# A decoder layer's MoE stage: the norm's per-feature factor moved from the token rows into the experts' gate and up weights

## The chip, the cores and the metric

The kernel runs on one core of a Trainium2 chip. The metric is device time in microseconds (us) of one execution, the median of several. The core has a matrix engine (TensorE, **PE** in the rows; its weight loads are **PEld**), a vector engine (VectorE, **DVE**), an activation engine (ScalarE, **ACT**), a general engine (GpSimd, **POOL**) and a queue that issues transfers (SyncE, **SP**); 16 DMA engines move data between device memory and the on-chip memories (SBUF, and PSUM for matmul results). Each engine executes its own list of instructions in order and waits on the others through semaphores.

## What is computed

A decoder layer on x (1024 tokens x 1024 features): two mixers in parallel (a convolution branch and forgetting attention), cross-attention into 256 memory tokens, then a mixture of 16 experts of which each token uses two. The change touches only the norm ahead of the experts and the experts' first matmuls:

```python
def rmsnorm(x, g):
    y = x * lax.rsqrt(jnp.mean(x * x, axis=-1, keepdims=True) + EPS)
    return y * g

# inside the layer
h = rmsnorm(x, norm_moe_g)                       # g: one factor per feature
g_star = argmax(softmax(h @ wg + bg))            # one of 4 groups
e_sel = (h @ we + be)[group g_star]              # its 4 experts, top 2 are used
a = jnp.einsum("nd,edf->nef", hf, w_gate)
b = jnp.einsum("nd,edf->nef", hf, w_up)
u = jax.nn.silu(a) * b * combine[..., None]
x = x + jnp.einsum("nef,efd->nd", u, w_down)
```

Since h = (x r) g with r one number per token and g one per feature, the factor g may stand on the rows of h or on the rows of w_gate and w_up.

## The kernel before, in words

Matmuls are made exact enough by splitting both operands: `split` (L132 to L138) writes a high part with ACT (`hi`, L134, optionally times `scale`) and the remainder `lo` with DVE (L138) or, for some weights, POOL (L136); `mm3` (L140 to L144) then issues three matmuls per tile. The order of each engine's list is made by a scheduler ahead of time, from the order in the code, priorities (`high_priority`) and explicit "issue after" marks; free buffers limit how far ahead something may stand.

The stages in order of time: the mixers, the output projection, cross-attention (`xa_q`, `xa_attend`, `xa_out`), then routing and experts. Tokens go in two halves of 512. `xa_out(n)` (L768) computes half n of the cross-attention output with eight weight tiles; it transposes the result back to token rows x3 (PE L781, ACT L783), and sums their squares (DVE L784). `rows_of` (L903) makes the norm's factor r from these sums (a chain of small DVE instructions, L907 and L165 to L150, called n3v, n3t, n3r), corrects the router's logits with it (L910, L911), and writes the normed rows to device memory. For the first half ACT multiplies x3 by r (L925) and POOL by the factors of the features, `grow` (L926); for the second half POOL multiplies by `grow` ahead of time (`gained`, L819, tiles hg) and ACT by r once it is known (L918). `route` then picks the experts (DVE L953 to L982, result M), places the tokens with small matmuls (PE L986 to L989), computes the slots of the tokens in each expert's list (Am on DVE, `slot_sums` on PE, L1081), and from these the indices `ids`. With `ids`, POOL issues the indirect transfers that gather an expert's rows (`fetch`, L1305); PE transposes them (L1251), ACT and DVE split the transposes (xgT), PE multiplies them with the split weights `gu` (L142 to L144).

Two experts, 0 and 1, are handled early: their first 128 rows come from the first half of the tokens alone, so that their matmuls can run while the second half is routed. The other 14 follow in a loop (L1490 on): load the raw weights (SP, L1407), split them (`gu_weights`, L1194, tiles of 128x1024; four for gate and up, two for down, per expert), gather, transpose, multiply, and add to the output by an indirect transfer (L1352). A short second list of each of these experts uses the unsplit weights: its transposes are copied by ACT (`turn`, L1316, tile xgL).

The router's weights `wr` already carry g (L876). The tile `grow` was filled by a transfer on POOL's queue (L880); its buffer is used again by `gfin`, the factors of the final norm, loaded by SP (L1512).

Of the kernel before, what the change touches and what calls it, by code (L numbers as in the profile page):

```python
# [7 lines left out]
F32 = mybir.dt.float32  # L8
# [8 lines left out]
P = 128  # L17
# [38 lines left out]
def half(n):  # L56
    return slice(n * HALF, n * HALF + HALF)


def blk(i):  # L60
    return slice(i * P, i * P + P)
# [3 lines left out]
def layer_kernel(ctx, tc, a, out, dbg=None):  # L65
# [700 lines left out]
    st, HG = {}, {}  # L766

    def xa_out(n):  # L768
# [19 lines left out]
        for m in range(KD):  # L788
# [5 lines left out]
            if m == 4:  # L794
                for k in range(4):
                    products(k)
                rows(0)
                if n:
                    HG[0] = gained(0)
# [10 lines left out]
        if n:  # L810
            HG[1] = gained(1)
        return ss

    def gained(b):

        tiles = [xt_p.tile([P, 2, HALF], F32, name=f"hg{b}", tag=("xt1a", "xt1b")[b], bufs=2) for _ in range(2)]
        hg = [x[:, i] for x in tiles for i in range(2)]
        for t in range(4):
            G.tensor_tensor(hg[t], x3[4 + t][:, half(b)], grow[:, half(b)], op=OP.mult)  # L819
        return hg  # L820
# [58 lines left out]
    grow = ro.tile([P, D], F32, name="grow", tag="grow", bufs=1)  # L879
    G.dma_start(grow, bcast_rows(a["moe_g_row"], D))  # L880
# [22 lines left out]
    def rows_of(hf, ss, htile=None):  # L903
# [10 lines left out]
        for i in range(H4):  # L914
            if hf:
                for b in range(2):
                    h = HG[b][i]
                    A.activation(h, h, AF.Copy, scale=r[:, i:i + 1])  # L918
                    nc.sync.dma_start(h3_dram[blk(t0 + i), half(b)], h)
                continue  # L920
            h = htile()
            if i in ():
                V.scalar_tensor_tensor(h, x3[t0 + i], r[:, i:i + 1], grow, op0=OP.mult, op1=OP.mult)
            else:
                A.activation(h, x3[t0 + i], AF.Copy, scale=r[:, i:i + 1])  # L925
                G.tensor_tensor(h, h, grow, op=OP.mult)  # L926
            nc.sync.dma_start(h3_dram[blk(t0 + i)], h)
# [266 lines left out]
    def gu_weights(src, tile_, raw_=raw_tile, parts=range(4), raws=None):  # L1194
        gu = [[], [], []]
        for b in parts:
# [6 lines left out]
            split(t[0], t[1], raw)  # L1203
# [24 lines left out]
    with pool("rows") as rw:  # L1228
# [7 lines left out]
        lg0 = rows_of(0, ss0, lambda: rw.tile([P, D], F32, name="h3s", tag="h3s", bufs=2))  # L1236
# [4 lines left out]
        with tc.high_priority(offset=600):  # L1241
            lg1 = rows_of(1, ss1)
# [65 lines left out]
    def turn(e, h):  # L1308
        if is_shared(e) and h == 1:
# [6 lines left out]
            A.activation(XT[e, h], pt, AF.Copy)  # L1316
# [194 lines left out]
    gfin = ro.tile([P, D], F32, name="gfin", tag="grow", bufs=1)  # L1511
# [212 lines left out]
```

## Time and profile before

| | before |
|---|---|
| median of 3 runs | 1228.31 us (1223.48 to 1232.91) |
| the profiled execution, own time | 1228.64 us |
| span in the profile | 1226.9 us |
| mean granted TensorE clock | 0.985 of full speed |
| busy: PE / DVE / ACT / POOL | 1159.0 (94%) / 843.0 (69%) / 629.3 (51%) / 404.5 us (33%) |

The span is the time in which the engines work; some 1.7 us of the execution lie around it. A busy engine is one that executes something; the engine with the largest share is where to look for the bound, and the stretches in which it is idle tell what it waited for. "Granted clock" is the share of TensorE's full clock (2.4 GHz) that it was given; 0.5 is 1.2 GHz. Rows of a timeline give the start, the duration, engine, line of the kernel, operation, output and inputs; brackets give the idle time of the engine just before, and what ended it.

### The profile page before, as it was taken

The page shows a single profiled execution, that of the slowest core. Times are in us where ns is not written, and L with a number is a line of the kernel's source. Part 1 is how long each engine was busy: PE and PEld are TensorE (multiplying, and loading weights), DVE is VectorE, ACT ScalarE, POOL GpSimd, SP SyncE. Part 2 cuts the span into 40 slices and gives each one's busy share as a digit, 9 for nine tenths or more (in the row PEclk, how much of TensorE's full clock was granted, in tenths as well). Part 3 has the DMA queues.
Part 4 walks back from the last instruction along what each step waited for, and adds up shares of the span by engine and source line. Part 5 has one row for each costly group of instructions (what it writes and reads, how often), then busy time and mean ns, then how long its engine had stood idle before and what let it go on. Part 6 is the DMA issues. An engine that isn't in the chain of part 4 may idle for free. (4 is left out here: it accounts for less than half of the span.)

```text
span 1226.9 us, 17120 instructions
## 1 busy us (share of the span) xinstructions
PE 1159.0 (94%) x6173; PEld 908.7 (74%) x6174; DVE 843.0 (69%) x1569; ACT 629.3 (51%) x1059; POOL 404.5 (33%) x276
## 2 busy tenths in 40 slices
PE   7999999999999999999999999999977898999995
PEld 3678887878877777788888788788754666667773
DVE  5499998653969787791235754755997784766665
ACT  6345664442646555471333342733742575767765
POOL 3327996221010100101012665273034133233433
PEclk9999999999999999999999999999998898999998
DMA  5211224136111111111343453144356889999967
GB/s 208 75 37 52 58 97 156 51 106 231 53 57 44 44 59 46 39 55 46 103 163 129 155 167 111 66 123 121 101 192 243 270 243 300 301 292 311 320 169 285
DMA packets 57467, 174.12 MB, mean 142 GB/s; under 512 B 7992, under 2 KB 11080, under 8 KB 57376
## 3 DMA queue, kind: packets, MB, share of 16 engines
q1 hardware_dynamic: 49680, 149.76, 36.5%
q0 software_dynamic: 7696, 23.20, 8.1%
q8 instruction: 51, 0.84, 0.3%
q14 instruction: 40, 0.33, 0.1%
HBM read 136.92 MB, written 36.01 MB: 141 GB/s over the span
## 5 line engine op out<-in xcount | busy, mean ns | idle before, releaser
L136 POOL TENSOR_TENSOR w_lo<-w_raw,w_hi 128x1024 fp32r<-128x1024 f32 x58 | 140.1, 2415 | 463.4 <-ACT w_hi L134 453.6
L144 PE MATMUL ps_lin<-hh,w_lo 128*128 128x512 f32 x560 | 221.4, 395 | 2.5 <-POOL w_lo L136 2.5
L142 PE MATMUL ps_lin<-hh,w_hi 128*128 128x512 f32 x560 | 223.0, 398 | 0.7 <-DVE u L357 0.6
L143 PE MATMUL ps_lin<-hl,w_hi 128*128 128x512 f32 x560 | 221.5, 396 | 0.0
L134 ACT ACTIVATE w_hi<-w_raw 128x1024 fp32r<-128x1024 f32 (+1 forms) x100 | 92.1, 921 | 201.0 <-PE ps_lin L143 169.1
L144 PEld LDWEIGHTS ps_lin<-hh,w_lo 128*128 128x128 f32 x560 | 105.3, 188 | 24.6 <-POOL w_lo L136 4.6
L142 PEld LDWEIGHTS ps_lin<-hh,w_hi 128*128 128x128 f32 x560 | 105.4, 188 | 23.3 <-issue 2.9
L143 PEld LDWEIGHTS ps_lin<-hl,w_hi 128*128 128x128 f32 x560 | 105.4, 188 | 21.5 <-issue 1.6
L379 DVE SCALAR_TENSOR_TENSOR ps_cva<-u,dw_w,ps_cva 128x1024 f32<-128x1024 f32 x90 | 111.6, 1280 | 0.5
L138 DVE SCALAR_TENSOR_TENSOR gu<-e_raw,gu 128x1024 fp32r<-128x1024 f32 x64 | 77.5, 1222 | 4.5 <-ACT gu L134 0.8
L375 POOL TENSOR_TENSOR oc<-oc,pj 128x512 f32<-128x512 f32 x60 | 75.8, 1303 | 8.8 <-ACT pj L374 8.7
L134 ACT ACTIVATE gu<-e_raw 128x1024 fp32r<-128x1024 f32 x64 | 67.4, 1058 | 8.0 <-PE ps_lin L144 7.4
L142 PE MATMUL ps_lin<-gu,xgT 128*128 128x512 f32 x144 | 58.8, 408 | 4.1 <-ACT xgT L134 4.1
L374 ACT ACTIVATE pj<-u,dw_w 128x512 f32<-128x512 f32 x60 | 42.4, 721 | 34.3 <-POOL oc L375 34.2
L138 DVE SCALAR_TENSOR_TENSOR dn<-d_raw,dn 128x1024 fp32r<-128x1024 f32 x32 | 39.0, 1225 | 27.8 <-ACT dn L134 24.0
L1305 POOL DMA_INDIRECT xg<-h_dram,ids x29 | 35.2, 1215 | 67.5 <-PE ps_sco L1081 24.3
L143 PE MATMUL ps_lin<-gu,xgT 128*128 128x512 f32 x144 | 57.4, 399 | 0.0
L560 ACT ACTIVATE sc<-sc,mns 128x128 f32<-128x128 f32 (+3 forms) x64 | 49.4, 772 | 15.6 <-DVE mns L556 15.0
L144 PE MATMUL ps_lin<-gu,xgT 128*128 128x512 f32 x144 | 57.0, 396 | 0.0
L138 DVE SCALAR_TENSOR_TENSOR pl<-ps_tra,ph 128x512 fp32r<-128x512 f32 (+1 forms) x80 | 49.1, 636 | 9.3 <-ACT ph L134 8.2
L134 ACT ACTIVATE ph<-ps_tra 128x512 fp32r<-128x512 f32 (+1 forms) x80 | 41.8, 552 | 23.3 <-PE ps_tra L573 22.5
L573 PE MATMUL ps_tra<-ident,sc 128*128 128x128 f32 x288 | 47.5, 274 | 4.1 <-DVE sc L563 4.1
(471 smaller groups left out, 2855.5 us busy)
## 6 DMA issues: line engine op xcount, KB each, us to landing
e_raw<-in_w_gu SPq DMA_DIRECT2D x64, 512.0 KB, 6.4
w_raw<-in_w_in SPq DMA_DIRECT2D x36, 512.0 KB, 3.7
d_raw<-in_w_dn SPq DMA_DIRECT2D x32, 512.0 KB, 9.6
w_raw<-in_w_out SPq DMA_DIRECT2D x16, 512.0 KB, 3.6
xT<-in_xT SPq DMA_DIRECT2D x16, 256.0 KB, 5.2
gc_dram<-gc SPq DMA_DIRECT2D x8, 512.0 KB, 4.0
gc<-gc_dram SPq DMA_DIRECT2D x8, 512.0 KB, 5.2
mc_dram<-gc SPq DMA_DIRECT2D x8, 512.0 KB, 2.8
```

The lines of the kernel that those rows point to most:

```text
L134: order["split"] = A.activation(hi, src, AF.Copy, scale=scale)
L136: G.tensor_tensor(lo, src, hi.bitcast(F32), op=OP.subtract)
L138: V.scalar_tensor_tensor(lo, src, scale, hi.bitcast(F32), op0=OP.mult, op1=OP.subtract)
L142: TE.matmul(ps, lh, rh, start=first, stop=False)
L143: TE.matmul(ps, lh, rl, start=False, stop=False)
L144: return TE.matmul(ps, ll, rh, start=False, stop=last)
L374: A.activation(pj, uj, AF.Copy, scale=dw_h[:, c, j:j + 1])
L375: G.tensor_tensor(co[c][:, ns], co[c][:, ns], pj, op=OP.add)
L379: V.scalar_tensor_tensor(sums, u[c][:, j:j + T], dw_h[:, c, j:j + 1], sums, op0=OP.mult, op1=OP.add)
L560: A.activation(sc[:, :nk], sc[:, :nk], AF.Exp, scale=-1.0, bias=mns[:, nch - 1:nch], accum_out=sm)
L573: TE.transpose(pt[:, s_], pr[i][:, blk(j)], ident)
L1305: G.indirect_dma_start(out=XG[e, h][:n], out_offset=None, in_=src, in_offset=bass.IndirectOffsetOnAxis(ap=idx, axis=0))
```

## The change

The rows of h are written without the feature factors, and the gate and up weights are multiplied by them while they are split. With this, POOL's multiplies by `grow` (L926, L819), the tile, its transfer and `gained` go. `gu_weights` now makes two splits of 128x512 with a scale (one number per partition, from `g_moe`) out of each 128x1024 split. The short lists, which use the unsplit weights, get the factor when their transposes are copied: by DVE, as a product, where ACT copied. `gfin` gets a tile of its own, so its load no longer waits for a buffer.

```diff
@@ -763,7 +763,7 @@
                 mm3(ps, (xv[0][:, m, blk(h)], xv[1][:, m, blk(h)]), (pT[0][:, m], pT[1][:, m]), m == 0, m == 1)
             split(o2[n][0][h], o2[n][1][h], ps)
 
-    st, HG = {}, {}
+    st = {}
 
     def xa_out(n):
 
@@ -795,8 +795,6 @@
                 for k in range(4):
                     products(k)
                 rows(0)
-                if n:
-                    HG[0] = gained(0)
         for k in range(4, KD):
             products(k)
         lt = xb.tile([P, 2, MEM], F32, name="lt", tag="pr", bufs=3).rearrange("p a b -> p (a b)")
@@ -807,17 +805,7 @@
             TE.transpose(pt[:, t], lt[:, blk(t)], ident)
         st[n] = ro.tile([P, 4, 20], F32, name="lg", tag="lg", bufs=2)
         V.tensor_reduce(st[n], pt.rearrange("p t (g c) -> p t c g", g=4)[:, :, 0:20], axis=AX.X, op=OP.add)
-        if n:
-            HG[1] = gained(1)
         return ss
-
-    def gained(b):
-
-        tiles = [xt_p.tile([P, 2, HALF], F32, name=f"hg{b}", tag=("xt1a", "xt1b")[b], bufs=2) for _ in range(2)]
-        hg = [x[:, i] for x in tiles for i in range(2)]
-        for t in range(4):
-            G.tensor_tensor(hg[t], x3[4 + t][:, half(b)], grow[:, half(b)], op=OP.mult)
-        return hg
 
     def row_tile(n):
         if n == 0:
@@ -876,8 +864,6 @@
         V.tensor_scalar(wr[:, k, 0:20], wr[:, k, 0:20], g_moe[:, k:k + 1], None, op0=OP.mult)
     rb = ro.tile([P, 20], F32, name="rb")
     G.dma_start(rb, bcast_rows(a["router_b"], 20))
-    grow = ro.tile([P, D], F32, name="grow", tag="grow", bufs=1)
-    G.dma_start(grow, bcast_rows(a["moe_g_row"], D))
     rev = ro.tile([P, 4], F32, name="rev")
     for i in range(4):
         V.memset(rev[:, i:i + 1], 4.0 - i)
@@ -900,7 +886,7 @@
     def b4(x, n=4):
         return x[:, :, None].to_broadcast([P, H4, n])
 
-    def rows_of(hf, ss, htile=None):
+    def rows_of(hf, ss, htile):
 
         t0 = H4 * hf
         s = ro.tile([P, H4], F32, name="ssum", tag="ssum", bufs=2)
@@ -912,18 +898,8 @@
         if "lg" in dbg:
             nc.sync.dma_start(dbg["lg"][:, t0:t0 + H4], lg)
         for i in range(H4):
-            if hf:
-                for b in range(2):
-                    h = HG[b][i]
-                    A.activation(h, h, AF.Copy, scale=r[:, i:i + 1])
-                    nc.sync.dma_start(h3_dram[blk(t0 + i), half(b)], h)
-                continue
-            h = htile()
-            if i in ():
-                V.scalar_tensor_tensor(h, x3[t0 + i], r[:, i:i + 1], grow, op0=OP.mult, op1=OP.mult)
-            else:
-                A.activation(h, x3[t0 + i], AF.Copy, scale=r[:, i:i + 1])
-                G.tensor_tensor(h, h, grow, op=OP.mult)
+            h = htile(i)
+            A.activation(h, x3[t0 + i], AF.Copy, scale=r[:, i:i + 1])
             nc.sync.dma_start(h3_dram[blk(t0 + i)], h)
         return lg
 
@@ -1200,7 +1176,8 @@
                 raw = raw_()
                 nc.sync.dma_start(raw, src[:, 2 * b:2 * b + 2])
             t = [tile_(i, b) for i in range(2)]
-            split(t[0], t[1], raw)
+            for j in range(2):
+                split(t[0][:, j], t[1][:, j], raw[:, j], scale=g_moe[:, 2 * b + j:2 * b + j + 1])
             for i, x in enumerate((*t, raw)):
                 gu[i] += [x[:, 0], x[:, 1]]
         return gu
@@ -1233,13 +1210,13 @@
         def raw_rows():
             return rw.tile([P, 2, HALF], F32, name="e_raw", tag="e_raw", bufs=2)
 
-        lg0 = rows_of(0, ss0, lambda: rw.tile([P, D], F32, name="h3s", tag="h3s", bufs=2))
+        lg0 = rows_of(0, ss0, lambda i: rw.tile([P, D], F32, name="h3s", tag="h3s", bufs=2))
         backs = [weights(0, *route(0, lg0))]
         gu0 = gu_weights(a["w_gu"][0], gu_tile(0), raw_rows, parts=(0, 1))
         W[1] = [gu_weights(a["w_gu"][1], gu_tile(1), raw_rows)]
         ss1 = xa_out(1)
         with tc.high_priority(offset=600):
-            lg1 = rows_of(1, ss1)
+            lg1 = rows_of(1, ss1, lambda i: xt_p.tile([P, D], F32, name="h3t", tag=("xt1a", "xt1b")[i % 2], bufs=2))
     xastack.close()
 
 
@@ -1313,7 +1290,7 @@
             pt = bank("tra", [P, KD, n])
             for k in range(KD):
                 TE.transpose(pt[:, k], XG[e, h][:n, blk(k)], ident[:n, :n])
-            A.activation(XT[e, h], pt, AF.Copy)
+            V.tensor_tensor(XT[e, h], pt, g_moe[:, :, None].to_broadcast([P, KD, n]), op=OP.mult)
         else:
             rows_in(XG[e, h], *XT[e, h])
 
@@ -1508,7 +1485,7 @@
         store(e, 0)
 
 
-    gfin = ro.tile([P, D], F32, name="gfin", tag="grow", bufs=1)
+    gfin = ro.tile([P, D], F32, name="gfin")
     nc.sync.dma_start(gfin, bcast_rows(a["final_g_row"], D))
     eps4 = ro.tile([P, 1], F32, name="eps4")
     V.memset(eps4, EPS / 4)
```

**POOL, from the last row norm of cross-attention's memory side to the first gathers.** oacc is a sum that PE needs (L707), w_lo the low part of a projection weight, h3s and hg the rows of the two halves, xg the gathered rows. Before:

```order
L880 DMA grow<-in_moe_g_row 128x1024
L698 TENSOR_TENSOR oacc<-oacc,osq 128x512
L885 IOTA tokhi 128x8
L887 IOTA toklo 128x1
L136 TENSOR_TENSOR w_lo<-w_raw,w_hi 128x1024
...
L926 TENSOR_TENSOR h3s<-h3s,grow 128x1024 x4
L819 TENSOR_TENSOR hg_8377<-x3r,grow 128x512 x2
L819 TENSOR_TENSOR hg_8378<-x3r,grow 128x512 x2
L1305 DMA xg<-h_dram,ids_7335 128x1024 x2
L819 TENSOR_TENSOR hg_8484<-x3r,grow 128x512 x2
L819 TENSOR_TENSOR hg_8485<-x3r,grow 128x512 x2
```

The same place of the changed kernel:

```order
L851 IOTA place 128x256
L866 DMA rb<-in_router_b 128x20
L871 IOTA tokhi 128x8
L873 IOTA toklo 128x1
L136 TENSOR_TENSOR w_lo<-w_raw,w_hi 128x1024
L698 TENSOR_TENSOR oacc<-oacc,osq 128x512
L836 MEMSET order__7337 128x1 x14
L136 TENSOR_TENSOR w_lo<-w_raw,w_hi 128x1024 x2
L1282 DMA xg<-h_dram,ids_7335 128x1024 x2
L1282 DMA xg<-h_dram,ids 128x1024 x2
```

The multiplies are gone, the first gathers (now L1282) follow the projections' last low part directly, and the sum oacc has moved behind one w_lo.

**ACT at the second half's norm.** xgT are the high parts of the early experts' transposed rows, hg and h3t the rows of the second half. Before:

```order
L134 ACTIVATE xgT_8534<-ps_tra 128x512
L918 ACTIVATE hg_8377<-hg_8377,n3r 128x512
L918 ACTIVATE hg_8484<-hg_8484,n3r 128x512
...
L918 ACTIVATE hg_8485<-hg_8485,n3r 128x512
L134 ACTIVATE xgT_8534<-ps_tra 128x512
L134 ACTIVATE xgT_8538<-ps_tra 128x512
L1094 ACTIVATE ge<-ge 128x16
L1095 ACTIVATE ex<-ex 128x4
L134 ACTIVATE xgT_8538<-ps_tra 128x512
L134 ACTIVATE gu_8576<-e_raw 128x1024
L134 ACTIVATE gu_8582<-e_raw 128x1024
```

Of the changed kernel:

```order
L134 ACTIVATE xgT_8524<-ps_tra 128x512 x2
L134 ACTIVATE xgT_8528<-ps_tra 128x512
L902 ACTIVATE h3t<-x3r,n3r 128x1024 x4
L134 ACTIVATE xgT_8528<-ps_tra 128x512
L134 ACTIVATE gu_8566<-e_raw,g_moe 128x512 x2
L134 ACTIVATE gu_8574<-e_raw,g_moe 128x512 x2
L1070 ACTIVATE ge<-ge 128x16
L1071 ACTIVATE ex<-ex 128x4
```

Three of the four transposes' copies now stand ahead of the norm's rows instead of one, and four multiplies of 128x1024 stand where eight of 128x512 stood.

**DVE at the end of the second half's norm.** xgT are the low parts of the transposed rows. Before:

```order
L150 SCALAR_TENSOR_TENSOR n3r<-n3t,n3r 128x4
L910 TENSOR_TENSOR lg<-lg,n3r 128x80
L138 SCALAR_TENSOR_TENSOR xgT_8535<-ps_tra,xgT_8534 128x512
L911 TENSOR_TENSOR lg<-lg,rb 128x80
L953 TENSOR_REDUCE m_8614<-lg 128x16
```

Of the changed kernel:

```order
L150 SCALAR_TENSOR_TENSOR n3r<-n3t,n3r 128x4
L138 SCALAR_TENSOR_TENSOR xgT_8525<-ps_tra,xgT_8524 128x512
L148 TENSOR_TENSOR n3t<-n3r 128x4
L138 SCALAR_TENSOR_TENSOR xgT_8525<-ps_tra,xgT_8524 128x512
L149 SCALAR_TENSOR_TENSOR n3t<-n3t,n3v 128x4
L150 SCALAR_TENSOR_TENSOR n3r<-n3t,n3r 128x4
L896 TENSOR_TENSOR lg<-lg,n3r 128x80
L138 SCALAR_TENSOR_TENSOR xgT_8529<-ps_tra,xgT_8528 128x512
L897 TENSOR_TENSOR lg<-lg,rb 128x80
L929 TENSOR_REDUCE m_8608<-lg 128x16
```

Three splits of transposed rows now lie inside the chain from the row sums to the logits, where one lay.

## Rows read from the trace of the kernel before

**Rows 1.** Busy time by stretch: us, then per engine busy (instructions), clock, DMA share, GB/s.
```profile
900.00:980.00 80.00, 59.48 (x346) 42.88 (x345) 65.24 (x226) 31.74 (x51) 26.44 (x18) 0.87 0.69 241
1020.00:1040.00 20.00, 15.15 (x75) 11.22 (x75) 8.11 (x11) 8.26 (x14) 7.64 (x5) 0.83 0.96 302
1060.00:1100.00 40.00, 40.00 (x215) 28.64 (x216) 26.62 (x31) 28.52 (x42) 12.88 (x9) 1.00 1.00 318
```
**Rows 2.** The same view in stretches of 5 us within the routing.
```profile
920.00:925.00 5.00, 4.08 (x22) 2.27 (x23) 3.32 (x19) 0.00 (x0) 0.00 (x0) 0.67 0.26 105
925.00:930.00 5.00, 5.00 (x46) 2.63 (x42) 3.47 (x17) 0.84 (x2) 0.00 (x0) 0.65 0.25 67
```
**Rows 3.** Waits of PE, 895 to 985: us in total, times, longest.
```profile
PE ps_tra L1251 <- DVE xgT L138: 5.6, 1, 5.6
PE ps_lin L142 <- ACT xgT L134: 4.1, 1, 4.1
PE ps_st L1027 <- DVE w L1108: 3.8, 1, 3.8
PE ps_lin L144 <- DVE w_lo L138: 3.1, 1, 3.1
```
**Rows 4.** Timeline of POOL, 903 to 945.
```profile
906.66 4.73 POOL L926 TENSOR_TENSOR h3s<-h3s,grow 128x1024 f32<-128x1024 f32 x2 [61.46 <-ACT h3s L925]
915.20 4.77 POOL L926 TENSOR_TENSOR h3s<-h3s,grow 128x1024 f32<-128x1024 f32 x2 [3.81 <-ACT h3s L925]
930.16 5.52 POOL L819 TENSOR_TENSOR hg<-x3r,grow 128x512 f32<-128x512 f32 x4 [10.20 <-ACT w_hi L134]
935.85 1.05 POOL L1305 DMA_INDIRECT xg<-h_dram,ids  x1 [0.17 <-issue]
940.36 4.93 POOL L819 TENSOR_TENSOR hg<-x3r,grow 128x512 f32<-128x512 f32 x4 [2.18 <-ACT x3r L783]
```
**Rows 5.** Timeline of DVE, 899 to 952, eight of its instructions.
```profile
901.57 0.16 DVE L165 TENSOR_SCALAR n3v<-ssum 128x4 f32<-128x4 f32 x1
...
907.55 1.61 DVE L958 TENSOR_TENSOR oh<-fm_s,fm_b 128x64 f32<-128x64 f32 x1
909.08 2.33 DVE L958 TENSOR_TENSOR ohg<-fm_s,fm_b 128x16 f32<-128x16 f32 x1
...
915.35 2.40 DVE L982 TENSOR_SCALAR B<-E,toklo 128x128 bf16<-128x128 f32 x1
...
925.54 0.16 DVE L1004 TENSOR_SCALAR ids<-ssum 128x2 int32<-128x2 f32 x1
...
942.90 1.19 DVE L165 TENSOR_SCALAR n3v<-ssum 128x4 f32<-128x4 f32 x1
...
949.42 0.23 DVE L958 TENSOR_TENSOR oh<-fm_s,fm_b 128x64 f32<-128x64 f32 x1
...
951.50 0.23 DVE L976 TENSOR_TENSOR M<-E 128x64 bf16<-128x64 f32 x1
```
**Rows 6.** Timeline of PE at the second half's last transposes and first placing matmul.
```profile
939.78 0.66 PE L781 MATMUL ps_sco<-ident,x2T 128*128 128x128 f32 x4 [0.17 <-DVE ss L784]
...
959.39 0.18 PE L986 MATMUL ps_sco<-start,ones_b 128*128 128x16 bf16 x1
```
**Rows 7.** Lines L134 and L138 by form: ns min/median/max, first and last start, forms.
```profile
L134 ACT ACTIVATE gu<-e_raw x64: 1045/1061/1067, 875.4 to 1171.7; 128x1024 fp32r<-128x1024 f32 x64
L134 ACT ACTIVATE h<-x2T,g_xa x16: 705/708/736, 708.0 to 829.9; 128x512 fp32r<-128x512 f32 x16
...
L138 DVE SCALAR_TENSOR_TENSOR gu<-e_raw,gu x64: 1214/1224/1226, 876.9 to 1172.8; 128x1024 fp32r<-128x1024 f32 x64
L138 DVE SCALAR_TENSOR_TENSOR h<-x2T,g_xa,h x16: 746/2386/2431, 708.7 to 830.6; 128x512 fp32r<-128x512 f32 x16
```
**Rows 8.** Timeline of POOL, 831 to 835.
```profile
831.25 1.28 POOL L698 TENSOR_TENSOR oacc<-oacc,osq 128x512 f32<-128x512 f32 x1 [1.13 <-ACT osq L697]
...
832.68 2.36 POOL L136 TENSOR_TENSOR w_lo<-w_raw,w_hi 128x1024 fp32r<-128x1024 f32 x1
```

## Prediction, made before the changed kernel was run

> **What bounds the kernel now.** I read the busy time by stretch first. In the expert loop PE is busy for all of its time: 40.00 of 40 us between 1060 and 1100, at the full clock [rows 1]. What is off PE's list of matmuls, and hidden there, is worth nothing. Between 900 and 980, the routing, PE is busy for 59.48 of 80 us, at a mean clock of 0.87, while DVE has 65.24 [rows 1]. Here time can be gained, so I read PE's waits of this stretch next. Four make up most of the idle time, and all end with DVE or ACT: 3.1 us for a low part w_lo, 3.8 us for w of L1108, 5.6 us for the low part of a transposed row tile, 4.1 us for a high part of one [rows 3]. After the first two the granted clock was 0.67 and 0.65 over ten microseconds in which PE had work nearly throughout [rows 2]: part of that time ran at 1.2 GHz in place of 2.4 GHz. So an idle stretch costs its length and some slow matmuls behind it.
>
> Then I read POOL and DVE side by side to see why DVE was late. Two POOL multiplies run from 906.66 for 4.73 us, that is to 911.39 [rows 4]. A DVE instruction of L958 that takes 0.23 us elsewhere took 1.61 us from 907.55, and its successor took 2.33 us from 909.08, to 911.41 [rows 5]: each ends when one of POOL's multiplies ends. The next pair of multiplies begins at 915.20 [rows 4], and an instruction of L982 that begins at 915.35 takes 2.40 us [rows 5]. In the second half's norm, n3v takes 1.19 us at 942.90 where the first half's took 0.16 [rows 5]; POOL multiplies from 940.36 for 4.93 us [rows 4]. The step behind it, L166, is of the same size and lies within the same POOL stretch. I read this as: some DVE instructions are held until POOL's current multiply ends. That POOL is in the way a second time shows in the gathers: the indices are ready at 925.54 [rows 5], but the gather is issued at 935.85, behind four multiplies that run from 930.16 [rows 4], which themselves waited for their rows.
>
> **The change, part by part.** *The multiplies go.* Three things follow. First, the hold in the first half: both of PE's waits, 3.1 + 3.8 = 6.9 us, are DVE work that stood behind held instructions. The clock's loss after them is worked out from the windows: 4.08 busy us at 0.67 and 5.00 at 0.65 lose 4.08 x 0.33 + 5.00 x 0.35 = 3.1 us. Together 10.0 us. Not all goes: without the hold DVE's chain of routing instructions is still there, and two of the low parts of a gate and up tile now stand inside it (2 x 0.75 us by the fastest row with such an operand [rows 7]), so PE will wait for M when it reaches the placing matmuls. I leave 1.0 us for this. **First half: -9.0**, between -7.5 and -10.
>
> Second, the other half's norm. From the end of PE's last transposes, 939.78 + 0.66 = 940.4, to its first placing matmul of this half, 959.39, pass 19.0 us [rows 6]. Before, two chains meet there: the sums, the norm and the routing on DVE (M ends at 951.50 + 0.23 = 951.7 [rows 5], 11.3 us after the transposes), and the early experts' transposed rows, which arrive late because of the gathers and whose copies on ACT stand behind eight multiplies. In the changed order three of the four copies stand ahead of the norm's rows, and the gathers, issued once the indices are there, land while PE still has projections. So only the DVE chain is left: 11.3 us, less 1.0 for each of two held instructions and 0.6 for a smaller hold, an estimate from the difference of 1.19 and 0.16 [rows 5], plus 1.4 for two more splits of transposed rows in the chain (about 0.7 us each). That makes 10.1, and the placing comes 8.9 us sooner. PE will still idle in this chain, and then run slowly for some microseconds; I take 0.9 off. **Second half: -8.0**, between -5 and -10.
>
> Third, the stores to device memory wait for no POOL product. No row of PE's waits hangs on them except through the gathers, counted already: 0.
>
> *What moves on POOL.* The sum oacc took 1.28 us from 831.25, and its own wait ahead of it was 1.13 us; the next low part took 2.36 us [rows 8]. In the changed order that low part stands ahead. Its input is there at about 830, so it ends near 832.4, and the sum ends at 833.7 in place of 832.5. PE's sum matmuls wait for it: **+1.2**.
>
> *The splits in halves.* A gate and up tile took ACT 1.06 us; two halves with an operand for the scale are 2 x 0.71 = 1.42 by the nearest rows, so +0.36 us. DVE: 1.22 before, 2 x 0.75 = 1.49 after, +0.27 us [rows 7]. (The larger median of h on DVE, 2.39 us, is the same hold: POOL is making low parts in that stage. It makes none in the expert loop, so I take the minimum.) There are 64 tiles, from 875 to 1173 [rows 7]: 23 us of ACT and 17 us of DVE in all. Fourteen experts' 56 tiles in the last 190 us are 12 in 40 us. That adds 4.3 us to ACT's 28.52 and 3.2 us to DVE's 26.62 [rows 1], 33 and 30 of 40. Both stay below PE, so PE hides it: 0 there. Right after the routing the first tiles are made just ahead of the matmuls that use them, and there I take six tiles' DVE price, **+1.6**, between 0 and 4.
>
> *The short lists' product.* Ten copies go from ACT to DVE: at about 0.5 us each some 5 us of DVE in all, in the loop, where PE covers them: 0. *gfin's load* moves from the middle of the down weights to the time before the output weights of cross-attention; half a megabyte, in a stretch where PE is covered by loads made well ahead: 0.
>
> **The sum.** -9.0 - 8.0 + 1.2 + 1.6 = -14.2 us. The profiled execution took 1228.64, so 1214.4; it lies 0.3 us above the median of the runs shown, 1228.31, which I ignore. By the bounds: -10 - 10 + 1.2 + 0 = -18.8 gives 1209.8, and -7.5 - 5 + 1.2 + 4 = -7.3 gives 1221.3.
>
> **The rivals.** *More is gained.* Between 1020 and 1040 PE was busy for 15.15 us at a clock of 0.83 [rows 1]: 4.85 us idle and about 15.15 x 0.17 = 2.6 us slow, all of one late gather. The routing of all experts comes nearly 17 us sooner and PE only 14, so transfers gain some time on PE. If the gap closes, 14.2 + 7.4 = 21.6: 1207. Against it: that gather's issue stands in POOL's list behind an addition to the output, which waits for the experts' own matmuls and shifts with them.
>
> *The hold isn't POOL's.* DVE may have been slow for another reason that was there at the same times (ACT was reading the same rows, transfers were writing). Then the first half's 9.0 stays, and of the second half's 8.0 the held 2.6 stay too; the gathers' part, 5.4, less 2.8 of losses, leaves 1226. For it: one stretch of POOL is always accompanied by ACT work on the same rows. Against it: the ends agree to 0.1 us in the pair at 909 and 911 [rows 4, 5].
>
> *Slower: the halves' price comes onto PE's path.* If PE waits for each tile, through ACT and DVE in series, an expert costs 4 x (0.36 + 0.27) = 2.5 us more, and 13 experts 33 us: 1247. If only one engine's price counts, 13 x 4 x 0.27 = 14: 1228.4. It decides from the point at which PE's first matmul of an expert waits for its low part; in the loop PE now has no idle time at all [rows 1], and ACT has 11 of 40 us free, which speaks against it. The Trainium skill ("ScalarE: Activation LUTs", section "What ACT_TABLE_LOAD costs") speaks for a real price: each instruction has a fixed part and each operand that is read per partition adds about 93 ns to it, so that cutting a tile in two pays the fixed part twice and the operand twice. By its figures a tile costs 0.28 us more on ACT, an estimate, where the nearest rows say 0.36; by that, ACT's total would rise by 18 us and not by 23, and the serial case would give 1243.
>
> **How the numbers follow.** The forecast has 0.52 (1210 to 1221, 1214.4 the likeliest); more gained 0.17 (1203 to 1210); the hold not POOL's, or most of the gain given back in the loop, 0.19 (1221 to 1228); the halves on the path 0.12 (1228 to 1247). About 1% is what a measurement of this kernel can tell from no change: below 1216.0 is faster, above 1240.6 slower. Of the forecast's 0.52 I put 0.33 below 1216; with 0.17 that is 0.50 faster. Slower is half of the last case, 0.06. The rest, 0.44, is within 1%. The range of 8 in 10 is 1205 to 1226: it leaves out the halves' case, the tail of the one before it and a little of the gains.
>
> **What would show it.** In the changed profile, the instructions of L958 and L982 and both n3v should be near 0.2 us, PE's two waits for w_lo and w should be gone and the clock near 1.00 from 905 to 925 by the old times. The first gathers should be issued within 2 us of their indices. From the last transposes to the placing there should be about 10 us. The wait for oacc should be near 1.8 us. In the loop PE should still be full. I am wrong if DVE shows the same long instructions without POOL, if PE waits for gate and up low parts in the loop, or if the gap near 1028 grows.

## The result and the profile after

| | before | after |
|---|---|---|
| median of 11 runs each | 1228.35 us (1220.97 to 1232.91) | 1219.14 us (1214.94 to 1224.41) |
| ratio | 1 | 0.9928 [0.9909, 0.9946] |
| the profiled execution, own time (span) | 1228.64 (1226.9) | 1214.94 (1213.2) |
| mean granted clock | 0.985 | 0.991 |

The changed kernel is 9.2 us faster, 0.7%. The forecast was 14.2 us. The profiled execution is the fastest of its eleven and gains 13.7 us: the forecast seems met there, but, as the later sections show, by luck, with terms that were wrong in opposite directions. Timed again beside other runs, the changed kernel had ratios of 0.997 [0.995, 0.999], 0.9951 [0.9931, 0.9972] and 0.9963 [0.9941, 0.9985]: 0.3 to 0.5%. The first of these, 1224.34 us, misses the 1219 that had been expected of it. So the gain is between 0.3 and 0.7%, 4 to 9 us, and that it is not nothing is clear in every comparison.

Busy time by stretch, changed kernel (columns as in [rows 1]; the third and fourth lines answer to [rows 2]):

```profile
900.00:980.00 80.00, 71.40 (x396) 51.91 (x395) 64.28 (x254) 41.48 (x68) 7.94 (x7) 0.94 0.79 274
1060.00:1100.00 40.00, 40.00 (x265) 29.05 (x265) 28.51 (x44) 30.62 (x49) 14.83 (x11) 1.00 0.96 304
920.00:925.00 5.00, 5.00 (x46) 3.40 (x43) 4.39 (x23) 1.72 (x3) 0.00 (x0) 1.00 0.21 53
925.00:930.00 5.00, 5.00 (x22) 3.22 (x22) 2.32 (x6) 0.00 (x0) 2.02 (x2) 1.00 0.91 303
```

In the routing PE is busy for 71.40 of 80 us where it was 59.48, and from 920 to 930 the clock is 1.00 where it was 0.67 and 0.65 at the same times. In the loop PE is still full, although DVE and ACT have more to do. PE's waits from 820 to 985 in the changed kernel:

```profile
PE ps_tra L1228 <- DVE xgT L138: 3.4, 1, 3.4
PE ps_tra L1228 <- DMA xg<-h_dram,ids: 3.4, 1, 3.4
PE ps_acc L707 <- POOL oacc L698: 2.4, 1, 2.4
```

The four large waits of [rows 3] have become two of 3.4 us. Those for w_lo and for w, 3.1 and 3.8 us, are gone, and so is ACT's of 4.1. Two waits that were small in the kernel before have grown, the one for a gather and the one for oacc. Before, in the same view:

```profile
PE ps_tra L1251 <- DMA xg<-h_dram,ids: 2.5, 2, 1.4
PE ps_acc L707 <- POOL oacc L698: 0.6, 1, 0.6
```

DVE's timeline shows the hold gone (L934 was L958 before, L958 was L982, L980 was L1004; compare [rows 5]):

```profile
910.47 0.22 DVE L934 TENSOR_TENSOR oh<-fm_s,fm_b 128x64 f32<-128x64 f32 x1
910.61 0.17 DVE L934 TENSOR_TENSOR ohg<-fm_s,fm_b 128x16 f32<-128x16 f32 x1
...
914.71 0.28 DVE L958 TENSOR_SCALAR B<-E,toklo 128x128 bf16<-128x128 f32 x1
...
920.50 0.17 DVE L980 TENSOR_SCALAR ids<-ssum 128x2 int32<-128x2 f32 x1
...
938.52 0.17 DVE L165 TENSOR_SCALAR n3v<-ssum 128x4 f32<-128x4 f32 x1
```

What took 1.61, 2.33, 2.40 and 1.19 us takes 0.22, 0.17, 0.28 and 0.17. From PE's timeline, the end of the second half's transposes and its first placing matmul (L962 was L986; compare [rows 6]):

```profile
935.99 0.66 PE L781 MATMUL ps_sco<-ident,x2T 128*128 128x128 f32 x4 [0.62 <-DVE ss L784]
...
946.89 0.18 PE L962 MATMUL ps_sco<-start,ones_b 128*128 128x16 bf16 x1
```

From 936.65 to 946.89 pass 10.2 us. Before it was 19.0, and the forecast was 10.1.

**Where the time went, as a ledger.** The same matmul of the same product stands in both traces. The difference of its start times says how far the changed kernel is ahead there: the transposes above began at 939.78 before [rows 6] and begin at 935.99 now, so PE is 3.8 us ahead. I took eight such matmuls at stage borders and list what each stretch between them brought (us, minus is a gain; the times are those of the kernel before, of which there is one profile). Besides the first profile there are three later profiles of the same changed kernel.

| stretch | forecast | after | again | third | fourth |
|---|---|---|---|---|---|
| 820 to 878: sum oacc behind a low part | +1.2 | +1.6 | +3.2 | +4.8 | +4.7 |
| 878 to 905 | 0 | +1.0 | +1.0 | +1.1 | +1.0 |
| 905 to 935: the hold, first half | -9.0 | -7.3 | -7.3 | -7.4 | -7.3 |
| 935 to 964: the second half's norm | -8.0 | -8.0 | -8.0 | -8.0 | -8.1 |
| 964 to 984: right after the routing | +1.6 | +4.1 | +4.4 | +4.1 | +4.5 |
| 984 to 1057: with the gap near 1028 | 0 | -6.4 | -0.4 | -2.3 | -6.4 |
| 1057 to 1190: expert loop | 0 | +0.3 | +0.3 | +0.3 | +1.2 |
| sum | -14.2 | -14.8 | -6.9 | -7.4 | -10.4 |

The middle rows come out within half a microsecond in every execution. Two rows vary: the one with oacc, and the one with the gap. In these four profiles they decide whether the sum looks like the forecast. (The table covers 820 to 1190 only. Ahead of it the executions differ by -1.2 to +2.1 us, and behind it the changed kernel gives back 0.2 to 2.1.)

### The profile page after: what moved, and what is told of

It reads as the page before. It is cut to its first block, busy times and chain, and to the rows that moved or that the text cites. A ratio compares the mean times of both kernels' runs of the same rounds, so it can differ in the third digit from the quotient of the medians.

```text
span 1213.2 us, 17223 instructions
## 1 busy us (share of the span) xinstructions
PE 1159.1 (96%) x6173; PEld 907.7 (75%) x6174; DVE 841.3 (69%) x1643; ACT 643.1 (53%) x1109; POOL 385.0 (32%) x263
## 4 chain that ended last, share of the span: by engine, by line
PE 67%; DVE 9%; POOL 8%; DMA 7%; ACT 6%; issue 3%; SPq 0%; ACTq 0%; DVEq 0%; POOLq 0%
PE ps_lin L142 15%; PE ps_lin L143 15%; PE ps_lin L144 15%; POOL oc L375 5%; PE ps_acc L589 3%; PE ps_tra L573 2%; DMA xg<-h_dram,ids 2%; POOL w_lo L136 2%; PE ps_sco L1347 2%; DMA e_raw<-in_w_gu 2%; DMA at<-attn_dram 2%; PE ps_tra L1228 1%; PE ps_sco L551 1%; PE ps_sco L552 1%; DVE kl L311 1%
## 5 line engine op out<-in xcount | busy, mean ns | idle before, releaser
L134 ACT ACTIVATE w_hi<-w_raw 128x1024 fp32r<-128x1024 f32 (+1 forms) x100 | 92.3, 923 | 190.4 <-PE ps_lin L143 149.3
L138 DVE SCALAR_TENSOR_TENSOR gu<-e_raw,g_moe,gu 128x512 fp32r<-128x512 f32 x128 | 90.1, 748 | 1.1 <-ACT gu L134 1.0
L134 ACT ACTIVATE gu<-e_raw,g_moe 128x512 fp32r<-128x512 f32 x128 | 85.2, 718 | 8.0 <-PE ps_lin L144 4.3
L1282 POOL DMA_INDIRECT xg<-h_dram,ids x29 | 35.2, 1213 | 147.2 <-DVE ssum L1060 78.3
L138 DVE SCALAR_TENSOR_TENSOR pl<-ps_tra,ph 128x512 fp32r<-128x512 f32 (+1 forms) x80 | 49.1, 636 | 9.3 <-ACT ph L134 8.3
L134 ACT ACTIVATE ph<-ps_tra 128x512 fp32r<-128x512 f32 (+1 forms) x80 | 41.8, 553 | 23.3 <-PE ps_tra L573 22.3
L142 PE MATMUL ps_lin<-mgh,w_hi 128*128 128x512 f32 x128 | 50.2, 392 | 0.9 <-DVE ga L640 0.9
```

The costliest lines, as they stand in the source:

```text
L134: order["split"] = A.activation(hi, src, AF.Copy, scale=scale)
L138: V.scalar_tensor_tensor(lo, src, scale, hi.bitcast(F32), op0=OP.mult, op1=OP.subtract)
L142: TE.matmul(ps, lh, rh, start=first, stop=False)
```

## The experiments

All were timed over five rounds against the kernel before on the same chip.

**1. Is the hold POOL's?** The kernel before, with POOL's twelve multiplies taken out and nothing else: the rows lack their feature factor.

```diff
-        for t in range(4):
-            G.tensor_tensor(hg[t], x3[4 + t][:, half(b)], grow[:, half(b)], op=OP.mult)
...
-                    A.activation(h, h, AF.Copy, scale=r[:, i:i + 1])
+                    A.activation(h, x3[t0 + i][:, half(b)], AF.Copy, scale=r[:, i:i + 1])
...
-                G.tensor_tensor(h, h, grow, op=OP.mult)
```

> The kernel before without POOL's twelve multiplies by grow (the rows of h miss the feature factors); the weights are split whole, as before. Hold by POOL (the forecast's mechanism): L958 and L982 near 0.2 us, no idle time of PE before w_lo and w, 8 to 13 us faster than before, 1215 to 1220. Rival, the hold is not POOL's: the long DVE instructions stay, and it is 2 to 5 us faster at most, by the earlier gathers, 1223 to 1226. PE's router matmuls (L775) stay in groups of four here, so if this beats the changed kernel by 3 us or more, the halves of the splits are what the changed kernel pays.

Measured: 1216.33 us (1213.25 to 1218.13), 0.9900 [0.9864, 0.9935]. DVE's timeline of this run (L955 is L958 of before):

```profile
910.01 0.23 DVE L955 TENSOR_TENSOR oh<-fm_s,fm_b 128x64 f32<-128x64 f32 x1
910.16 0.17 DVE L955 TENSOR_TENSOR ohg<-fm_s,fm_b 128x16 f32<-128x16 f32 x1
...
934.07 0.17 DVE L165 TENSOR_SCALAR n3v<-ssum 128x4 f32<-128x4 f32 x1
```

With ACT and the transfers at their old work on the same rows, the held instructions are short. The hold is POOL's; the rival "the hold isn't POOL's" falls. In the ledger the stretch from 905 to 935 brings 10.7 us here: just above the forecast's upper bound for the hold, 10, and 3.4 more than in the changed kernel. So something in the changed kernel takes 3.4 us back in this stretch. As a whole, run 1 is 8.0 us below the changed kernel on the same chip (1224.34, experiment 3): that is what the rest of the change costs beside the departure of the multiplies.

**2. What do the halves cost?** The kernel before, with only the splits in halves added: rows and weights both carry the factor here, so it enters twice.

```diff
-            split(t[0], t[1], raw)
+            for j in range(2):
+                split(t[0][:, j], t[1][:, j], raw[:, j], scale=g_moe[:, 2 * b + j:2 * b + j + 1])
```

> The kernel before with only the splits of gate and up in halves with a scale (the factor is applied twice in the full lists). Theory formed from the changed profile: the price is paid by PE, not by ACT or DVE: the longer splits pull the router's matmuls L775 out of their groups of four, each lone one takes about 1 us of PE, four more groups make +4 us, 1231 to 1234. Forecast's own: PE hides it, 1228 to 1230. Rival, on PE's path in every expert: 1242 or more, with PE waiting for gu in the loop.

Measured: 1230.55 us (1225.15 to 1237.64), 1.0023 [0.9995, 1.005]. This lies between the two ranges written down, and the interval does not tell them apart. The busy time in the loop, and PE's wait for a gather from 930 to 990, of this run:

```profile
1060.00:1100.00 40.00, 40.00 (x220) 28.43 (x217) 28.06 (x42) 30.83 (x52) 12.88 (x9) 1.00 1.00 309
```

```profile
PE ps_tra L1252 <- DMA xg<-h_dram,ids: 5.0, 1, 5.0
```

The loop's price is hidden: 0.5 us from 1057 on, and PE is full. The rival "the halves on PE's path", 1228 to 1247 on the change as a whole and at least 14 us for the halves, falls. But the halves alone cost 1.1 us from 878 to 905, as in the changed kernel, and 2.8 from 905 to 935. From 964 to 984 they cost 4.8, after a gain of 5.8 in the stretch before, and the long wait for a gather that the changed kernel has stands here too. In the kernel before it was 1.4 us at the longest, in run 1 it was 1.0.

**3. Lone router products.** Between run 1 and the changed kernel one thing caught the eye, the router's products (L775): eight per half, each two matmuls with 32 output columns, four column blocks side by side. PE's timeline of them, for the second half, in run 1:

```profile
919.32 1.06 PE L775 MATMUL ps_st<-x2T,wr 128*32 128x512 f32 x8
...
927.57 1.90 PE L775 MATMUL ps_st<-x2T,wr 128*32 128x512 f32 x8
```

and in the changed kernel:

```profile
916.89 1.04 PE L775 MATMUL ps_st<-x2T,wr 128*32 128x512 f32 x2
...
918.09 1.06 PE L775 MATMUL ps_st<-x2T,wr 128*32 128x512 f32 x6
...
923.18 1.04 PE L775 MATMUL ps_st<-x2T,wr 128*32 128x512 f32 x2
...
925.39 1.05 PE L775 MATMUL ps_st<-x2T,wr 128*32 128x512 f32 x2
...
931.41 1.05 PE L775 MATMUL ps_st<-x2T,wr 128*32 128x512 f32 x2
...
932.98 1.04 PE L775 MATMUL ps_st<-x2T,wr 128*32 128x512 f32 x2
```

Four products that follow one another take 1.06 us together, three take 1.06, and one alone takes 1.04. (In the row of 1.90 us the last product waited for its rows and ran alone behind the other three.) The Trainium skill ("TensorE: Matmul & The Clock Gate", section "Part 3: Packing small matmuls — row/col tiling") has it that products of 32 columns that land in different column blocks run at the same time; the row of 1.06 us for four agrees. The changed order put other matmuls between them: six pieces, 6.3 us, where run 1 has 1.06 + 1.90 = 3.0. That is 3.3 us. (The kernel before has two groups as well, 1.94 + 1.90 = 3.8 us, the first of them at the clock of 0.65 of [rows 2]; against it the second half's products take 2.4 us more.) It is the halves that go with the scattering: in run 2 the second half's products stand in five pieces, and the first half's take 4.1 us, as in the changed kernel, where the kernel before and run 1 have 3.2. Four of the six pieces, 4.2 us, lie between 905 and 935, where run 1 has one of 1.06: by the rows, 3.1 of the 3.4 that were missing. To see it directly, I held the products of both halves back until their group is complete:

```diff
-            TE.matmul(ps_st[c], wr[:, m], x2[n][m], start=m < 4, stop=m >= 4)
+            return TE.matmul(ps_st[c], wr[:, m], x2[n][m], start=m < 4, stop=m >= 4)
...
-                for k in range(4):
-                    products(k)
+                with tc.issue_after(made.ins):
+                    for k in range(4):
+                        products(k)
...
-        for k in range(4, KD):
-            products(k)
+        with tc.issue_after(products(KD - 1).ins):
+            for k in range(4, KD - 1):
+                products(k)
```

(`made` is the last matmul of the fifth weight tile.) It ran beside the changed kernel:

> The changed kernel with the router's matmuls L775 of the second half held back until four can go together. If lone ones cost 1 us of PE each, four groups less give 3 to 4 us, 1215 to 1216. Rival, they fill time in which PE would wait anyway for the routing: no change, 1219.

> The changed kernel, unchanged, for a second profile. Its runs lie between 1215 and 1224 and the profiled one was the fastest. If the gap for the late gather near 1028 by the old times varies between executions, a slower execution shows it again (5 to 7 us); if the spread is in the mixers' stages, the loop is the same and the time before 900 differs. Median expected 1219.

Measured: 1220.06 us (1215.56 to 1223.48), 0.9926 [0.99, 0.9952], against 1224.34, 0.997 [0.995, 0.999], for the changed kernel on the same chip: 4.3 us less. PE's timeline of the products in the grouped run:

```profile
923.82 1.06 PE L775 MATMUL ps_st<-x2T,wr 128*32 128x512 f32 x8
...
933.14 1.07 PE L775 MATMUL ps_st<-x2T,wr 128*32 128x512 f32 x8 [0.35 <-DVE x2T L793]
```

Two pieces, 2.1 us, where there were 6.3: 4.2 us less work in the second half, and 1.1 less in the first by the ledger (-0.1 from 878 to 905); 4.3 of these 5.3 are seen in the medians. In the ledger 905 to 935 brings 8.8 in place of 7.3, and 964 to 984 loses 1.4 in place of 4.4, so part of the gain appears only there. That is, of the 3.4 us that were missing from 905 to 935 the grouping gives back 1.5, here and in every later run with it; the other 1.9 are not shown to be the products'.

**4. The sum oacc.** In the changed kernel a low part stands ahead of it on POOL:

```profile
830.38 2.40 POOL L136 TENSOR_TENSOR w_lo<-w_raw,w_hi 128x1024 fp32r<-128x1024 f32 x1 [0.26 <-ACT w_hi L134]
832.73 1.71 POOL L698 TENSOR_TENSOR oacc<-oacc,osq 128x512 f32<-128x512 f32 x1
```

The sum ends at 834.44 where it ended at 832.53 [rows 8], and PE waits 2.4 us for it where it waited 0.6. That wait is 2.4 us in the later profiles too, but the stretch costs 3.2 to 4.8 there. The windows around the wait, of the first profile, of the second ("again") and of the third, and a shorter one behind it in the third:

```profile
832.00:850.00 18.00, 15.59 (x73) 13.02 (x73) 6.74 (x38) 3.95 (x6) 7.76 (x18) 1.00 0.47 135
832.00:850.00 18.00, 15.59 (x66) 12.51 (x65) 8.14 (x42) 4.26 (x7) 8.78 (x18) 0.91 0.50 139
832.00:850.00 18.00, 16.99 (x65) 14.07 (x66) 5.05 (x29) 3.09 (x4) 6.29 (x17) 0.81 0.35 115
835.00:840.00 5.00, 5.00 (x13) 3.84 (x13) 3.39 (x24) 0.23 (x1) 0.43 (x13) 0.50 0.44 164
```

The clock is 1.00, 0.91 and 0.81 here (0.81 in the fourth profile too). So in some executions the wait is followed by a stretch at 1.2 GHz, 0.50 in the last row, and the order of these clocks is that of the costs in the ledger: 1.6, 3.2, 4.8 and 4.7. The low parts were put behind the sum again:

```diff
-                G.tensor_tensor(acc, acc, sq, op=OP.add)
+                order["oacc"] = G.tensor_tensor(acc, acc, sq, op=OP.add)
...
-            w = wtile(a["xa_wq"][h], lo_eng=G)
+            with tc.issue_after(order["oacc"].ins) if n and h else nullcontext():
+                w = wtile(a["xa_wq"][h], lo_eng=G)
```

> The changed kernel with the later cross-attention query weights' splits held back until POOL's last sum oacc is issued, so that the sum stands ahead of the low part as in the kernel before. PE's wait for oacc 0.6 us in place of 2.4, and no stretch at half the clock behind it: 2 to 3.5 us faster than the changed kernel on the same chip. Rival, the idle time moves to the low part that is now later: no change.

> The changed kernel with both: the router's matmuls of the second half in groups of four, and the sum oacc first. If the two losses are independent, 5.5 to 7.5 us faster than the changed kernel, 11 to 14 us faster than before, about what the kernel without POOL's multiplies gave (0.99). If what is left of the difference is the price of the halves elsewhere, it stays 2 us or more above that one.

> The changed kernel, unchanged, on the same chip as the two others: 1219 to 1225. In its profile, either the gather near 1018 lands within 5 us and PE has no gap, or it takes 7 us or more and PE waits about 4 us and then runs at half the clock.

Measured on one chip: 1216.71 us, 0.9911 [0.9878, 0.9945], with the sum first; 1215.70 us, 0.9906 [0.9876, 0.9935], with this and the grouping; 1221.14 us, 0.9951 [0.9931, 0.9972], for the changed kernel. So the sum first gives 4.4 us, about what the third profile shows in its row of the ledger (4.8), and more than the 2 to 3.5 that I had expected. PE's waits from 820 to 985 with both repairs:

```profile
PE ps_tra L1231 <- DMA xg<-h_dram,ids: 1.6, 1, 1.6
...
PE ps_acc L707 <- POOL oacc L698: 0.8, 1, 0.8
```

The wait for the sum is 0.8, and the stretch from 820 to 878 costs nothing (-0.1). The two repairs together give 5.4 us (5.2 in the session below), less than 4.3 + 4.4 and a little less than the 5.5 to 7.5 expected. Whether they share a wait or the medians of different sessions do not add up is not shown.

**5. The wait after the routing.** The changed kernel's DVE timeline there (L969 was L993, the reduction that the second half's slots need):

```profile
948.25 2.73 DVE L138 SCALAR_TENSOR_TENSOR gu<-e_raw,g_moe,gu 128x512 fp32r<-128x512 f32 x4
950.90 0.28 DVE L969 TENSOR_REDUCE q<-tm 128x8 f32<-128x128 f32 x1
...
953.95 0.17 DVE L985 TENSOR_SCALAR ids<-ssum 128x4 int32<-128x4 f32 x1
```

Four halves of expert 0's splits stand ahead of q, which is in the chain to the indices (ids) and so to the gather that PE waits for. The theory: they delay the gather by their 2.7 us. For the experiment the last two gate and up tiles of expert 0 were split only after the routing's last step on DVE:

```diff
-                V.tensor_scalar(Am[:, i, t], place, q[:, i, t:t + 1], None, op0=OP.is_equal)
+                order["am"] = V.tensor_scalar(Am[:, i, t], place, q[:, i, t:t + 1], None, op0=OP.is_equal)
...
-        gu0 = [x + y for x, y in zip(gu0, gu_weights(a["w_gu"][0], gu_tile(0), parts=(2, 3)))]
-        W[0] = (gu0, dn_weights(a["w_dn"][0]))
+        for b in (2, 3):
+            raws0[b] = raw_tile()
+            nc.sync.dma_start(raws0[b], a["w_gu"][0][:, 2 * b:2 * b + 2])
...
+    with tc.issue_after(order["am"].ins):
+        gu0 = [x + y for x, y in zip(gu0, gu_weights(None, gu_tile(0), parts=(2, 3), raws=raws0))]
+    W[0] = (gu0, dn_weights(a["w_dn"][0]))
```

> The changed kernel with the four low-part halves of expert 0's last two weight tiles issued on DVE after the second half's Am, so that q follows tm directly as before (in the changed kernel 3.3 us of splits stand between them, and PE later waits 3.4 us for a gather). If that is where the 4 us between 964 and 978 by the old times go, PE's wait for that gather falls to 1 us or less: 2 to 4 us faster than the changed kernel. Rival, the late down weights of expert 0 hold PE there anyway: no change.

> All three repairs: the sum oacc first, the router's matmuls of the second half in groups of four, q and Am ahead of the split halves. If the losses are independent, 8 us or more faster than the changed kernel and 13 to 17 us faster than before; if they share one wait, no better than the two repairs alone.

> The kernel with two repairs once more, beside the one with three: 1212 to 1218, and 4 to 7 us faster than the changed kernel.

> The changed kernel, unchanged, on the same chip: 1219 to 1225; the wait for oacc is 2.4 us in every profile, with half a clock behind it in some.

Measured on one chip: 1223.32 us, 0.9947 [0.9928, 0.9966], with the routing first; 1221.96, 0.9963 [0.9941, 0.9985], for the changed kernel; 1216.80, 0.9912 [0.9879, 0.9944], with the two repairs again; 1215.59, 0.9914 [0.9882, 0.9947], with all three. The routing first gives nothing, with the other repairs or without. DVE's timeline with the routing first:

```profile
948.59 0.28 DVE L969 TENSOR_REDUCE q<-tm 128x8 f32<-128x128 f32 x1
...
950.92 2.73 DVE L138 SCALAR_TENSOR_TENSOR gu<-e_raw,g_moe,gu 128x512 fp32r<-128x512 f32 x4
...
954.37 0.17 DVE L985 TENSOR_SCALAR ids<-ssum 128x4 int32<-128x4 f32 x1
```

The order was turned round: q comes 2.3 us sooner. The indices come no sooner: the same 2.7 us of halves now stand between the routing and the sum that yields them, PE's slot sums begin at 953.19 in place of 952.85 although their input Am is ready 1.9 us sooner, and the stretch costs 3.8 us. So the experiment did not bring the gather forward, and the theory that these halves delay it is neither shown nor refuted. With all three repairs the kernel is 6.4 us below the changed one, where 8 or more had been expected if the losses were independent.

The traces answer the question in another way: the gather is not slower than it was. Before (POOL, then PE), and in the changed kernel:

```profile
969.61 0.97 POOL L1305 DMA_INDIRECT xg<-h_dram,ids  x1 [24.32 <-PE ps_sco L1081]
...
972.92 0.39 PE L144 MATMUL ps_lin<-dn,ul 128*128 128x512 f32 x1
974.73 1.09 PE L1251 MATMUL ps_tra<-ident,xg 128*128 128x128 f32 x8 [1.42 <-DMA xg<-h_dram,ids]
```

```profile
954.86 0.95 POOL L1282 DMA_INDIRECT xg<-h_dram,ids  x1 [26.96 <-DVE ul L138]
...
960.10 1.97 PE L1228 MATMUL ps_tra<-ident,xg 128*128 128x128 f32 x8 [3.38 <-DMA xg<-h_dram,ids]
...
963.03 0.79 PE L142 MATMUL ps_lin<-dn,uh 128*128 128x512 f32 x1 [0.54 <-ACT uh L134]
```

From the gather's issue to the transposes of its rows pass 5.1 us before and 5.2 now. What changed is the order of PE's rows: from the first placing matmul to these transposes PE had 12.9 us of work before, the first nine matmuls with the down weights (dn) and sixteen slot sums among it, and 9.8 now; that work stands behind the transposes, so PE waits with it undone. Run 1 has the old order (a wait of 0.5 at this place), run 2 and every run with the halves have the dn matmuls behind the transposes. Behind the wait the clock is 0.50 from 960 to 965 and 0.83 from 965 to 970; in the kernel before it is 1.00 from 970 to 985. So the halves bring this wait by way of PE's order. Why the scheduler chose it (the later splits of the down weights, or something else) stays open, and no run here puts the old order back.

**6. The gap near 1028.** It needed no kernel of its own: the profiles of the same changed kernel differ. The busy time from 1020 to 1060 in the first profile:

```profile
1020.00:1060.00 40.00, 39.27 (x195) 27.15 (x193) 29.70 (x43) 31.52 (x52) 12.56 (x8) 1.00 1.02 327
```

and in the second ("again"), with the wait in it from PE's timeline:

```profile
1020.00:1060.00 40.00, 35.95 (x183) 25.63 (x183) 24.27 (x37) 23.95 (x42) 12.93 (x9) 0.91 0.96 285
```

```profile
1027.32 1.73 PE L1228 MATMUL ps_tra<-ident,xg 128*128 128x128 f32 x7 [4.05 <-DMA xg<-h_dram,ids]
```

The gather that PE waits for here, in POOL's timeline of the first profile and of the second:

```profile
1013.85 1.14 POOL L1282 DMA_INDIRECT xg<-h_dram,ids  x1 [0.30 <-PE ps_lin L144]
```

```profile
1018.18 1.14 POOL L1282 DMA_INDIRECT xg<-h_dram,ids  x1 [0.30 <-issue]
```

In the second it lands at 1027.19, 9.0 us after its issue, and PE goes on at 1027.32. In the first it lands after 5.7 us, and no wait of PE for it is left. Both run with the transfer engines full (0.96 and 1.02). In the third and the fourth profile it takes 8.5 and 5.2 us; the gap closes in the first and the fourth. It closes in one of two profiles with both repairs too, and did not in run 1. I found nothing in the program that decides it. So it is a spread of some 6 us between executions of one and the same kernel. The kernel before has one profile, with the gap and 9.2 us for this gather; whether the change makes the gap close more often is not shown.

## Why the prediction was right in sum, and where its steps failed

**Right: what bounds the kernel, and the hold.** The multiplies' departure makes the held instructions short (experiment 1), both waits of the first half go and the clock returns to 1.00, as the windows show. In run 1, where nothing else changes, this is worth 10.7 us, beyond the forecast's 9.0 and just above its bound of 10. The Trainium skill ("GPSIMD Engine Reference", section "8. Key points") says that POOL shares its ways into the local memory with DVE, and that DVE instructions with two inputs there, or in a mode that uses two ports, contend. The trace agrees with it on one kind: oh has two inputs and was held for 1.61 us [rows 5]. B and n3v were held with one large input each; in which mode they ran, no row here shows. How long the hold lasts is seen in the rows: the end of the held instruction is the end of POOL's multiply (909.08 + 2.33 = 911.41 for ohg, 906.66 + 4.73 = 911.39 for the multiplies [rows 4, 5]).

**Right: the second half.** Forecast -8.0 and 10.1 us from the transposes to the placing; measured -8.0 to -8.1 and 10.2. The forecast's reason has a part that the multiplies' departure alone does not give: in run 1 this stretch brings 2.8 us, and PE's wait for ACT's copy of a transposed row tile, 4.1 us before [rows 3], is still 4.3 there. In the changed kernel, where three copies stand ahead of the norm's rows on ACT, it is gone. That fits the forecast's second chain, and no run separates it from the rest of the change.

**Right: the loop.** The halves take 718 and 748 ns on ACT and DVE in the mean, twice that per tile, as forecast from the nearest rows (2 x 0.71 and 2 x 0.75). The groups in the changed kernel's page:

```profile
L138 DVE SCALAR_TENSOR_TENSOR gu<-e_raw,g_moe,gu 128x512 fp32r<-128x512 f32 x128 | 90.1, 748 | 1.1 <-ACT gu L134 1.0
L134 ACT ACTIVATE gu<-e_raw,g_moe 128x512 fp32r<-128x512 f32 x128 | 85.2, 718 | 8.0 <-PE ps_lin L144 4.3
```

PE is full from 1060 to 1100 all the same, and the loop costs 0.3 us in three profiles of four.

**Wrong: work that became longer by being scattered.** The forecast left the router's products out of the sum altogether. They take 0.9 to 1.0 us more than in the kernel before in the first half (878 to 905) and 2.4 more in the second, or 3.3 more than in run 1, where both halves run at the full clock. The forecast for the first half had looked at DVE and POOL alone, where the waits were, and took PE's work as given; but the order of PE's rows had changed as well. The scattered work is the same in all four profiles; of what it costs, grouping gave back 4.3 us.

**Mis-sized: the sum oacc.** +1.2 was forecast; the wait grew by 1.8 (2.4 for 0.6), since the low part ended at 832.78 in place of 832.4 and the sum itself took 1.71 in place of 1.28, and in three profiles of four a lower clock behind it brought the cost to 3.2 to 4.8. The forecast counted this loss of clock for the waits that went, and not for the one that came.

**Wrong in its reason: right after the routing.** +1.6 was forecast, with 4 as its bound; measured 4.1 to 4.5. The six tiles' own price on DVE was taken. What the rows show is PE's order again: the matmuls that filled the wait for a gather now stand behind it, so the wait is 3.4 us in place of 1.4, with the slow clock behind it (experiment 5).

**Luck: the gap near 1028.** The rival that it closes held in two profiled executions of four. It had been written as one outcome of the change, and it varies with the execution.

**The marks that were named.** Held instructions near 0.2 us, the two waits gone, clock 1.00, PE full in the loop: seen. The wait for oacc near 1.8 us: it is 2.4. The first gathers within 2 us of their indices: not so. The indices are there at 920.50, and the gather is issued at 925.58, in POOL's timeline:

```profile
925.58 1.05 POOL L1282 DMA_INDIRECT xg<-h_dram,ids  x1 [78.33 <-DVE ssum L1060]
```

By this row POOL waited there for a DVE sum (ssum) that comes later than the indices, not for multiplies. It cost PE nothing that the rows show.

In sum: 1219.1 lies inside the range and in the forecast's own case (1210 to 1221). The likeliest value was 4.7 us too low. In the four profiles the steps of the sum missed by 5.9 to 10.2 us together: oacc and the clock behind it by 0.4 to 3.6, the first half by 2.7 (the scattered products and 1.9 us that are not explained, less a hold that was worth 1.7 more than forecast), the stretch after the routing by 2.5 to 2.9, the loop by 0.3 to 1.2. The gap near 1028, which was in no term, gave back 0.4 to 6.4. So the first profile's 14.8 for 14.2 is luck. By the bound of 1% the result is "no change" and not "faster", which had been given 0.44 and 0.50.

**A version that beats both.** Changed kernel, products grouped, sum first: 1215.70 and 1216.80 us in two sessions, ratios of 0.9906 [0.9876, 0.9935] and 0.9912 [0.9879, 0.9944] to the kernel before, some 5 us below the changed kernel on the same chips, and within the intervals the ratio of run 1, 0.9900, whose rows lack the factor.

## What to carry to other kernels

When a change lets a scheduler reorder an engine that is the bound, read its rows too: instructions that run side by side only when they stand side by side can cost several times as much when scattered (four products: 1.06 us together, 1.04 each alone), without any wait to show for it, and matmuls that filled a wait can come to stand behind it. Price a wait that you add as you price one that you remove, with the slow clock behind it. And take the profile of more than one execution before you read a gap late in the program as an effect of the change.

## What the runs showed of the hardware

- DVE instructions that take 0.17 to 0.28 us by themselves took 1.19 to 2.40 us when they ran beside a POOL multiply, and ended with it (911.41 and 911.39).
- Products of 32 output columns in different column blocks: four in 1.06 us, three in 1.06, one in 1.04.
- The same idle time of PE, 2.4 us, was followed by full clock in one execution and by a window at 0.50 in another.
- A gather of the same place in the program, with the transfer engines full, landed 9.0 us after its issue in one execution and held PE up, and after 5.7 us in another, without a wait of PE.
